# Norm weights spread into PSUM by TensorE, one-value operations as tensor_scalar, and one product for branch B's meta tokens

## The chip, the cores and the metric

The kernel runs on one core of a Trainium2 chip. The core has TensorE (matmul; its weight loads are shown as an engine of their own), VectorE (DVE), ScalarE (ACT), GpSimd (POOL) and SyncE, whose queue (SP) issues most of the transfers from and to the chip's memory. The metric is the device time of one execution in microseconds (us); a kernel's time is the median of several runs.

## The reference

One layer of a bidirectional encoder: 16 meta tokens are put ahead of 1024 tokens of width 1024; the rows are normalised, projected into ten blocks of columns, run through two attention branches, gated, mixed and normalised again. Cut to what the change touches:

```python
def rmsnorm(x, g):
    y = x * lax.rsqrt(jnp.mean(x * x, axis=-1, keepdims=True) + EPS)
    return y * g

h = concatenate([meta_tokens, x])                      # 16 + 1024 rows
hn = rmsnorm(h, pre_norm_g)
qa, ka, va, za, qb, kb, vb, zb, ga, gb = split(hn @ w_in + b_in)
oa = diff_attention(qa, ka, va, ...)                   # branch A: dense, 4 heads, two maps each
ob = windowed_gqa(qb, kb, vb, ...)                     # branch B: each block of 128 queries sees 3 blocks of keys
ya = (oa * silu(za)) @ w_out_a
yb = (ob * silu(zb)) @ w_out_b
h = h + rmsnorm((sigmoid(ga) * ya + sigmoid(gb) * yb) @ w_out, post_norm_g)
return h[16:]
```

In branch B only the first block of queries has the 16 meta tokens among its keys.

## The kernel before

All products keep fp32 accuracy by splitting operands into a rounded high part (fp32r) and the remainder: `hi*hi + hi*lo + lo*hi`. The weight splits run on POOL (L139, L140 in `load_w`), the splits of activations on ACT (high part) and DVE (remainder).

**Start.** The nine row blocks (block 0, block 1, the meta tokens as block -1, then 2 to 7) are each loaded by the SP queue (`load_x`, `ld` at L116), normalised (`norm_block`) and transposed (`turn_block`). `norm_block` squares on ACT with a row sum (L237), works out one value per row in `rstd` (sqrt on ACT at L161; on DVE L162 and L163, then L164 and L165 as `scalar_tensor_tensor` on 128x1 tiles) and applies it with the weights in one DVE pass over 128x1024 (L239). The weights `gb` are a 128x1024 tile in SBUF that one broadcast transfer of 512 KB fills. `turn_block` transposes eight 128x128 pieces on TensorE (L251) into two PSUM tiles (pool `psT` for the first four, `psS` for the others), and ACT (L254) and DVE (L255) write the parts into `hn`. Meanwhile `prepare` and `tables` make the bias tables (L272 on POOL, L283 on TensorE into `psS` banks, L284 on ACT).

**First projections.** As row blocks become ready, `k_proj`, `v_proj` and `q_proj` of branch B take chunks of columns: K and V in chunks of 264, 264, 256 and 256, Q in two of 512. Each chunk is 24 products (L151) into one bank of the two-bank pool `psmm`, then an evacuation (K: two ACT passes L328 and two DVE passes L332; V: one ACT pass L347; Q: L309 to L313). The row work has priority over the projections in the order that is laid out for each engine; that order is fixed when the kernel is built, and each engine follows its own in order. PSUM has eight banks: `psmm` 2, `psT` 2, `psV` 1, `psS` 3. An x tile is one of five buffers, and the load of a later block waits until the L239 pass of an earlier one has read its buffer.

**Branch B.** For each of four pairs of heads and eight query blocks: scores, softmax, transposes (`b_trans`, L432), and the value products (`b_values`, L445), six a step: three key blocks, each with the high and the low part of the probabilities. For query block 0 the third key block is the 16 meta rows, held in `VBM`, 16 partitions.

**After it.** Branch A (L585 to L629), in which L629 multiplies an 80-row tile `am` by an 80-row `VM` whose unused rows are zero, so that one product covers the meta rows' high and low parts; then gates, mixing, and the output stage, whose eight row blocks call `rstd` again (after the one-value sums L1056 and L1062). In branch A L596 is a one-value `tensor_tensor` once a step, 32 in all.

Of the kernel before, what the change touches and what calls it, by code (L numbers as in the profile page):

```python
# [17 lines left out]
P = 128  # L18
# [60 lines left out]
def _body(ctx, tc, A, out, dbg, stop):  # L79
# [35 lines left out]
    def ld(o, i):  # L115
        return sp.dma_start(o, i)  # L116
# [42 lines left out]
    def rstd(ss, st, n=P):  # L159

        act.activation(st[:n, 0:1], ss, AF.Sqrt, scale=4.0 / D, bias=eps4[:n])  # L161
        dve.tensor_scalar(st[:n, 3:4], ss, -4.0 / D, -4.0 * EPS, ALU.mult, ALU.add)  # L162
        dve.reciprocal(st[:n, 1:2], st[:n, 0:1])  # L163
        dve.scalar_tensor_tensor(st[:n, 4:5], st[:n, 1:2], st[:n, 3:4], st[:n, 1:2], ALU.mult, ALU.mult)  # L164
        dve.scalar_tensor_tensor(st[:n, 2:3], st[:n, 4:5], 3.0, st[:n, 1:2], ALU.add, ALU.mult)  # L165
        return st[:n, 2:3]
# [25 lines left out]
    VB_ = vt()  # L192
    VBM = sbp.tile([MT, 2, P], F32R, tag="am", name="vbm", bufs=1)
    xts = {}
# [13 lines left out]
    pool.memset(rb[32:33], 1.0)  # L208
    oh = [sbp.tile([33, LT // 2], F32, tag="U", name="oh") for _ in range(2)]
    load_x(0)  # L210
    act.dma_start(rb[:32], A["rel_bias"])
# [3 lines left out]
    load_x(-1)  # L215
    gb = sbp.tile([P, D], F32, tag="Q", name="gb", bufs=2)
    ld(gb, A["pre_norm_g"].partition_broadcast(P).rearrange("p o d -> p (o d)"))

# [13 lines left out]
    def norm_block(b):  # L232
        n = MT if b < 0 else P
        xt = xts.pop(b)
        xs = sbp.tile([P, D], F32, tag=("ah", "al")[b % 2], name="xs")
        st = sbp.tile([P, 8], F32, tag="st", name="st", bufs=9)
        pins[act] = act.activation(xs[:n], xt[:n], AF.Square, accum_out=st[:n, 5:6])  # L237
        r = rstd(st[:n, 5:6], st, n)
        pins[dve] = dve.scalar_tensor_tensor(xs[:n], xt[:n], r, gb[:n], ALU.mult, ALU.mult)  # L239
        xss[b] = xs  # L240
# [34 lines left out]
    def tables():  # L275
        for j in range(2):
            hot = hots[j]
            tab = sbp.tile([12, half], F32, tag="U", name="tab")
            for s in range(0, half, 512):
                w = min(512, half - s)  # L280
                pb = psS.tile([P, 512], F32, tag="s", name="pb")
                for x in range(2):
                    pe.matmul(pb[:12, :w], lhsT=rbs[:, x], rhs=hot[:, s:s + w], start=(x == 0), stop=(x == 1))  # L283
                act.activation(tab[:, s:s + w], pb[:12, :w], AF.Copy, scale=8.0)  # L284
            act.dma_start(tab_d[:, j * half:(j + 1) * half], tab)
# [4 lines left out]


    def zeros(*x):
        z = sbp.tile([P, 256], F32, tag="sq", name="zero", bufs=1)[:80]
        pool.memset(z, 0.0)
        for y in x:
            pool.tensor_scalar(y, z[:, :y.shape[1]], 1.0, 1.0, ALU.mult, ALU.mult)

    vm = [sbp.tile([80, P], F32R, tag=f"vm{j}", name=f"vm{j}", bufs=1) for j in range(2)]

    def masks():  # L300
        zeros(*vm)
        onesm = sbp.tile([P, 256], F32, tag="sq", name="onesm", bufs=1)[:, :P]
        pool.memset(onesm, 1.0 / P)
        pool.tensor_scalar(onesr, onesm, 1.0, 1.0, ALU.mult, ALU.mult)

    def q_proj(col, Q, w=None):
        def evac(ps, st, n, b):
            o = st - MT
            act.activation(Q[:64, 0, o:o + n], ps[:64, :n], AF.Identity, bias=b[:64])  # L309
            act.activation(Q[64:, 1, o:o + n], ps[64:, :n], AF.Identity, bias=b[64:])  # L310
            dve.scalar_tensor_tensor(Q[64:, 0, o:o + n], ps[:64, :n], b[:64], Q[:64, 0, o:o + n],
                                     ALU.add, ALU.subtract)
            dve.scalar_tensor_tensor(Q[:64, 1, o:o + n], ps[64:, :n], b[64:], Q[64:, 1, o:o + n],  # L313
                                     ALU.add, ALU.subtract)
        yield from proj(col, QCH, evac, w)

    def k_proj(col, KH, KL, w=None):
# [6 lines left out]
        def evac(ps, st, n, b):  # L324
# [10 lines left out]
            if w is not None and st + n in (SPLIT, C):  # L335
                copies(st + n - 512 - MT * (st < SPLIT), st + n)
        yield from proj(col, KCH if w is None else KCH4, evac, w)
        if w is None:
# [3 lines left out]
    def v_proj(col, put, w=None):  # L342
# [7 lines left out]
        yield from proj(col, KCH if w is None else KCH4, evac, w)  # L350
        for b0, nb, rows in ((0, 4, P), (4, 4, P), (8, 1, MT)):
# [20 lines left out]
    def put_b(VB):  # L372
        def put(pt, b0, nb, rows):
            for g in range(2):
                src = pt[:, :, 64 * g:64 * g + 64]
                v = VB[g][:, b0:b0 + nb] if b0 < 8 else VBM[:, g:g + 1]
                hi = v[:, :, :64]
                act.activation(hi, src, AF.Copy)
                dve.tensor_tensor(v[:, :, 64:], src, hi, ALU.subtract)
        return put  # L380
# [39 lines left out]
    def b_trans(i, sb):  # L420
        ah = sbp.tile([P, 4, 256], F32R, tag="ah", name="ah")
        al = sbp.tile([P, 4, 256], F32R, tag="al", name="al")
        if i == 0:
            blocks = ((17, P, 0), (17 + P, P, 1), (1, MT, 8))
        else:
            blocks = tuple((1 + P * j, P, i - 1 + j) for j in range(3 if i < NB - 1 else 2))
        for x in range(0, len(blocks), 2):
            pt = psT.tile([P, 2, 256], F32, tag="pT", name="pT")
            sub = blocks[x:x + 2]
            for y, (o, rows, _) in enumerate(sub):  # L430
                for j in range(2):
                    pe.transpose(out=pt[:rows, y, j * P:(j + 1) * P], in_=sb[:, j, o:o + rows], identity=ident)  # L432
            rows, n = sub[0][1], len(sub)
            act.activation(ah[:rows, x:x + n], pt[:rows, :n], AF.Copy)
            dve.tensor_tensor(al[:rows, x:x + n], pt[:rows, :n], ah[:rows, x:x + n], ALU.subtract)
        return ah, al, blocks

    def b_values(i, ah, al, blocks, g, ob):
        VB = VB_[g]
        pv = psV.tile([P, 512], F32, tag="pv", name="pv")  # L440
        n, last = 0, 2 * len(blocks) - 1
        for a in (ah, al):
            for x, (_, rows, blk) in enumerate(blocks):
                v = VB[:rows, blk, :] if blk < 8 else VBM[:, g, :]
                pe.matmul(pv[:, :256], lhsT=v, rhs=a[:rows, x, :], start=(n == 0), stop=(n == last))  # L445
                n += 1

        t = sbp.tile([P, 256], F32, tag="sq", name="bt", bufs=1)[:64]
# [126 lines left out]
    def a_scores(i, Q, KH, KL, U, fill):  # L575
# [104 lines left out]

    am = sbp.tile([80, 256], F32R, tag="am", name="am", bufs=1)
    zeros(am)
    U = a_table(0)
# [340 lines left out]
    with tc.tile_pool(name="fp", bufs=2, side="right", reuse_waits="tile") as fp:  # L1024
# [4 lines left out]
        def out_pair(p):  # L1029
# [13 lines left out]
            def result(o, v, cs):  # L1043
# [17 lines left out]
                if last:  # L1061
                    dve.tensor_tensor(s[:, 5:6], s[:, 5:6], s[:, 8:9], add)  # L1062
                if sqrt[0]:
# [44 lines left out]
```

## Time and profile before

| | us |
|---|---|
| median of 3 runs | 909.49 (909.27 to 910.65) |
| the profiled execution | 907.95 |
| its span on the core | 906.1 |
| TensorE busy in the span | 858.2 (95%) |
| DVE busy | 680.0 (75%) |
| ACT busy | 488.8 (54%) |
| POOL busy | 380.4 (42%) |

The span is what the trace covers; the profiled execution took 1.85 us more than its span. An engine counts as busy while an instruction of its own is in progress, and that includes time in which the instruction is held up inside the engine. In the page's 40 slices of 22.7 us TensorE is below 90% in four only: the first two, the one from 566 us, and the last.

### The profile page before, as it was taken

Reading aid. Unit: us, or ns where it says so; the run is one execution under the profiler, and the core shown is the slowest. Engines: PE = TensorE matmul, PEld = TensorE weight load, DVE = VectorE, ACT = ScalarE, POOL = GpSimd, SP = SyncE. Lnnn points to the kernel's source line nnn. Section 1 sums busy time; section 2 is a strip of 40 time slices with the busy share of each in tenths; the row PEclk is TensorE's granted clock in tenths of the full one; section 3 lists DMA queues with packets and bytes.
Section 4 is the critical chain, followed back from the end, with each engine's and each line's share of the span. In section 5 each row is a group of like instructions: output and inputs, shape, how many; then the busy total and the mean of one; then the engine's idle time right before and its main releaser. Section 6 shows DMA issues by size and latency. Waiting matters only on the chain.

```text
span 906.1 us, 13766 instructions
## 1 busy us (share of the span) xinstructions
PE 858.2 (95%) x4670; PEld 733.9 (81%) x4670; DVE 680.0 (75%) x1432; ACT 488.8 (54%) x975; POOL 380.4 (42%) x482
## 2 busy tenths in 40 slices
PE   4799999999999999999999999399999999999995
PEld 2797988888888898899888887288888888887784
DVE  6735668767988988997877699975444476959897
ACT  4635567766868768877766532344444540114432
POOL 6224543545021212221222189555454555826553
PEclk9999999999999999999999999699999999999998
DMA  8321110215122121021111153464511366311223
GB/s 262 105 50 45 56 57 19 89 43 133 36 71 68 47 72 68 25 71 48 47 65 48 47 185 117 163 210 161 178 56 47 131 231 207 94 63 47 94 95 138
DMA packets 64318, 85.85 MB, mean 95 GB/s; under 512 B 5248, under 2 KB 49294, under 8 KB 64248
## 3 DMA queue, kind: packets, MB, share of 16 engines
q1 hardware_dynamic: 56640, 60.28, 21.1%
q10 hardware_dynamic: 7576, 24.67, 7.9%
q8 instruction: 37, 0.61, 0.3%
q14 instruction: 33, 0.27, 0.1%
q0 software_dynamic: 32, 0.02, 0.0%
HBM read 60.63 MB, written 19.00 MB: 88 GB/s over the span
## 4 chain that ended last, share of the span: by engine, by line
PE 63%; DVE 21%; ACT 7%; issue 5%; POOL 1%; DMA 1%; SPq 0%; DVEq 0%; ACTq 0%; POOLq 0%
PE mm L151 21%; PE pp L862 17%; PE pp L966 9%; PE pv L627 3%; DVE sb L588 3%; PE pv L445 2%; PE pT L432 2%; PE pT L615 2%; PE s L585 2%; DVE sb L598 2%; ACT sb L591 2%; PE s L586 2%; ACT sb L597 1%; DVE ws L837 1%; DVE TB L885 1%
## 5 line engine op out<-in xcount | busy, mean ns | idle before, releaser
L151 PE MATMUL mm<-hn,wh 128*128 128x512 f32 (+2 forms) x896 | 203.6, 356 | 2.9 <-ACT vT L347 1.9
L139 POOL TENSOR_SCALAR wh<-wr 128x256 fp32r<-128x256 f32 x124 | 63.5, 528 | 265.9 <-PE mm L151 237.4
L151 PEld LDWEIGHTS mm<-hn,wh 128*128 128x128 f32 x896 | 145.1, 192 | 19.2 <-ACT vT L347 2.1
L140 POOL TENSOR_TENSOR wl<-wr,wh 128x256 fp32r<-128x256 f32 x124 | 107.4, 890 | 19.4 <-PE mm L151 17.4
L151 PE MATMUL mm<-hn,wl 128*128 128x512 f32 (+2 forms) x448 | 101.5, 353 | 0.0
L792 POOL TENSOR_TENSOR wl<-ws,wh 128x512 fp32r<-128x512 f32 x48 | 71.6, 1501 | 66.0 <-ACT wh L791 52.2
L591 ACT ACTIVATE sb<-sb,st 128x1040 f32<-128x1040 f32 x64 | 74.3, 1162 | 35.2 <-DVE st L588 34.4
L862 PE MATMUL pp<-t,wh 128*128 128x512 f32 (+1 forms) x296 | 73.2, 390 | 15.6 <-ACT wh L791 15.6
L862 PE MATMUL pp<-hn,wh 128*128 128x512 f32 x320 | 79.8, 391 | 0.0
L151 PEld LDWEIGHTS mm<-hn,wl 128*128 128x128 f32 x448 | 73.7, 191 | 7.6
L862 PEld LDWEIGHTS pp<-t,wh 128*128 128x128 f32 x296 | 55.5, 191 | 28.2 <-ACT wh L791 16.9
L588 DVE CUSTOM_DVE_ANT_0 sb<-s,U,st 128x346 f32<-128x346 f32 x128 | 73.1, 574 | 5.8
L871 DVE TENSOR_TENSOR c<-c,pp 128x512 f32<-128x512 f32 x70 | 47.4, 682 | 38.5 <-PE pp L862 36.7
L862 PEld LDWEIGHTS pp<-hn,wh 128*128 128x128 f32 x320 | 60.1, 188 | 13.2
L585 PE MATMUL s<-K,Q 128*128 128x346 f32 (+1 forms) x192 | 65.8, 345 | 0.9 <-DVE st L588 0.4
L586 PE MATMUL s<-K,Q 128*128 128x346 f32 (+1 forms) x192 | 61.3, 321 | 0.0
L598 DVE SCALAR_TENSOR_TENSOR sb<-sb,st 128x1040 f32<-128x1040 f32 x32 | 43.9, 1372 | 13.2 <-ACT sb L597 12.9
L413 ACT ACTIVATE sb<-sb,st 128x385 f32<-128x385 f32 (+2 forms) x64 | 37.5, 588 | 22.6 <-DVE st L410 20.3
L417 POOL TENSOR_SCALAR sb<-sb,st 128x384 f32<-128x384 f32 (+2 forms) x64 | 35.5, 568 | 32.5 <-DVE st L415 32.4
L791 ACT ACTIVATE wh<-ws 128x512 fp32r<-128x512 f32 x48 | 29.7, 625 | 35.0 <-PE pp L862 20.1
L410 DVE CUSTOM_DVE_ANT_0 sb<-s,TB,nsink 128x384 f32<-128x384 f32 (+2 forms) x64 | 35.4, 580 | 16.6 <-PE s L408 15.0
L617 DVE TENSOR_TENSOR al<-pT,ah 128x512 fp32r<-128x512 f32 x64 | 43.7, 686 | 3.6 <-ACT ah L616 2.9
(212 smaller groups left out, 1928.7 us busy)
## 6 DMA issues: line engine op xcount, KB each, us to landing
wr<-in_w_in_dram SPq DMA_DIRECT2D x96, 128.0 KB, 2.5
wr<-in_w_in_dram SPq DMA_DIRECT2D x16, 512.0 KB, 3.6
K<-K ACTq DMA_DIRECT2D x16, 260.0 KB, 3.5
xt<-in_x_dram SPq DMA_DIRECT2D x8, 512.0 KB, 7.1
sg_d<-TB ACTq DMA_DIRECT2D x8, 512.0 KB, 2.6
w<-in_w_out_dram SPq DMA_DIRECT2D x4, 1024.0 KB, 5.5
room<-sg_d SPq DMA_DIRECT2D x8, 512.0 KB, 4.8
fx<-in_x_dram SPq DMA_DIRECT2D x8, 512.0 KB, 4.6
```

Of the source, the lines that this page charges most:

```text
L139: pool.tensor_scalar(hi, raw, 1.0, 1.0, ALU.mult, ALU.mult)
L140: pool.tensor_tensor(lo, raw, hi, ALU.subtract)
L151: pe.matmul(ps[:, :n], lhsT=w[k // 4][:, k % 4, :], rhs=hslice(part, k, st, n), start=(i == 0), stop=(i == 3 * KC - 1))
L585: pe.matmul(s, lhsT=q, rhs=KH[:, m, o:o + n], start=True, stop=False)
L586: pe.matmul(s, lhsT=q, rhs=KL[:, m, o:o + n], start=False, stop=True)
L588: dve.tensor_tensor_reduce(out=sb[:, o:o + n], in0=s, in1=back(U, u0 + o, n), scale=-0.125, scalar=lim, op0=ALU.add, op1=ALU.min, accum_ou ...
L591: act.activation(sb, sb, AF.Exp, bias=st[:, m:m + 1], scale=-1.0, accum_out=st[:, 2 + m:3 + m])
L598: dve.scalar_tensor_tensor(sbs[0], sbs[0], st[:, 4:5], sbs[1], ALU.mult, ALU.add)
L792: lo_eng.tensor_tensor(t[1][:, k], x, t[0][:, k], sub)
L862: pe.matmul(x[n][:, cs], lhsT=w[:, k], rhs=b[n][part][:, k, cs], start=(i == 0), stop=(i == 11))
L871: dve.tensor_tensor(x[o][:, cs], *src, add)
L966: pe.matmul(py, lhsT=w[:, k, :], rhs=g[h][:, k], start=(i == 0), stop=(i == 11))
```

## The change

Four things change.

1. The weights of the first norm are loaded as one row of 4 KB (on ACT's queue, ahead of the other loads of that queue), split on DVE into a high and a low part, and spread over the 128 partitions by four TensorE products with a row of ones, into the two `psmm` banks, which they keep until the last norm. L239 becomes two passes of 512 columns that read the weights from PSUM. The table products move from `psS` to the one bank of `psV`, and the first projections (`beside(w)`) take their banks from `psS` instead of `psmm`.
2. L164 and L165 in `rstd`, L596, L1056 and L1062 become `tensor_scalar` with the second and third value as scalars per partition.
3. Branch B's meta rows are kept twice in an 80-row `VBM` (rows 0 to 15 and 64 to 79, zeros between) and the probabilities' high and low parts in the matching rows of `am`, so that one product replaces two. The value tile is written by twice as many small ACT and DVE passes, once.
4. `am` and `VBM` are zeroed in `masks` with the others, and no longer `am` ahead of branch A.

```diff
-        dve.scalar_tensor_tensor(st[:n, 4:5], st[:n, 1:2], st[:n, 3:4], st[:n, 1:2], ALU.mult, ALU.mult)
-        dve.scalar_tensor_tensor(st[:n, 2:3], st[:n, 4:5], 3.0, st[:n, 1:2], ALU.add, ALU.mult)
+        dve.tensor_scalar(st[:n, 4:5], st[:n, 1:2], st[:n, 3:4], st[:n, 1:2], ALU.mult, ALU.mult)
+        dve.tensor_scalar(st[:n, 2:3], st[:n, 4:5], 3.0, st[:n, 1:2], ALU.add, ALU.mult)
...
-    VBM = sbp.tile([MT, 2, P], F32R, tag="am", name="vbm", bufs=1)
+    VBM = sbp.tile([80, 2, P], F32R, tag="sh", name="vbm", bufs=1)
...
+    grow = sbp.tile([1, D], F32, tag="Q", name="grow", bufs=2)
+    act.dma_start(grow, A["pre_norm_g"])
...
-    gb = sbp.tile([P, D], F32, tag="Q", name="gb", bufs=2)
-    ld(gb, A["pre_norm_g"].partition_broadcast(P).rearrange("p o d -> p (o d)"))
+    one = sbp.tile([1, P], F32, tag="sq", name="one", bufs=1)
+    dve.memset(one, 1.0)
+    oner = sbp.tile([1, P], F32R, tag="vm0", name="oner", bufs=1)
+    dve.tensor_copy(oner, one)
+    gr = sbp.tile([1, 2, T], F32R, tag="Q", name="gr", bufs=2)
+    dve.tensor_copy(gr[:, 0], grow)
+    dve.tensor_tensor(gr[:, 1], grow, gr[:, 0], ALU.subtract)
+    gb = [psmm.tile([P, 512], F32, tag="mm", name="gb") for _ in range(2)]
+    for h in range(2):
+        for x in range(2):
+            pe.matmul(gb[h], lhsT=oner, rhs=gr[:, x, 512 * h:512 * h + 512], start=(x == 0), stop=(x == 1))
...
-        pins[dve] = dve.scalar_tensor_tensor(xs[:n], xt[:n], r, gb[:n], ALU.mult, ALU.mult)
+        for h in range(2):
+            c = slice(512 * h, 512 * h + 512)
+            pins[dve] = dve.scalar_tensor_tensor(xs[:n, c], xt[:n, c], r, gb[h][:n], ALU.mult, ALU.mult)
...
-                pb = psS.tile([P, 512], F32, tag="s", name="pb")
+                pb = psV.tile([P, 512], F32, tag="pv", name="pb")
...
+    def beside(w):
+        return {"room": lambda: psS.tile([P, 512], F32, tag="s", name="mm")} if w else {}
...
-        yield from proj(col, KCH if w is None else KCH4, evac, w)
+        yield from proj(col, KCH if w is None else KCH4, evac, w, **beside(w))
...
+        if i == 0:
+            pe.matmul(pv[:, :256], lhsT=VBM[:, g, :], rhs=am, start=False, stop=True)
...
-        dve.tensor_tensor(st[:, 6:7], st[:, 5:6], neglam, ALU.mult)
+        dve.tensor_scalar(st[:, 6:7], st[:, 5:6], neglam, None, ALU.mult)
...
-                    dve.tensor_tensor(s[:, 5:6], s[:, 6:7], s[:, 7:8], add)
+                    dve.tensor_scalar(s[:, 5:6], s[:, 6:7], s[:, 7:8], None, add)
```

## Rows read from the trace of the kernel before

**Rows 1.** Windows of the start: busy us of each engine, instructions, granted clock, DMA.

```profile
10.00:20.00 10.00, 8.32 (x29) 4.27 (x30) 9.96 (x16) 5.11 (x11) 9.09 (x13) 1.00 0.74 248
...
30.00:41.50 11.50, 9.65 (x64) 9.41 (x64) 9.90 (x29) 9.35 (x22) 0.00 (x0) 1.00 0.42 121
```

**Rows 2.** TensorE's waits from 41.5 to 240 us: us in total, times, longest.

```profile
PE mm L151 <- ACT vT L347: 1.9, 1, 1.9
```

**Rows 3.** Chain of waits, first 50 us: start us, us, what.

```profile
2.11 6.80 DMA gb<-in_pre_norm_g_dram
...
17.09 5.51 DVE st L164
...
22.82 1.28 DVE xs L239
...
30.00 4.49 PE mm L151 x19
```

**Rows 4.** Timeline of POOL, 12 to 23 us, first and last of eight rows.

```profile
12.14 1.73 POOL L139 TENSOR_SCALAR wh<-wraw 128x256 fp32r<-128x256 f32 x2
...
21.18 1.40 POOL L140 TENSOR_TENSOR wl<-wraw,wh 128x256 fp32r<-128x256 f32 x2
```

**Rows 5.** Timeline of DVE, 0 to 32 us.

```profile
3.88 0.17 DVE L268 CAST rbs<-rb 33x12 fp32r<-33x12 f32 x1 [3.88 <-DMA rb<-in_rel_bias_dram]
...
12.21 4.12 DVE L239 SCALAR_TENSOR_TENSOR xs<-xt,st,gb 128x1024 f32<-128x1024 f32 x2
16.25 0.13 DVE L162 TENSOR_SCALAR st<-st 128x1 f32<-128x1 f32 x1
16.32 0.67 DVE L255 TENSOR_TENSOR hn<-pt,hn 128x512 fp32r<-128x512 f32 x1
```

**Rows 6.** Timeline of TensorE, start.

```profile
11.86 1.88 PE L283 MATMUL pb<-hot,rbs 33*12 33x512 f32 x4
...
30.00 3.01 PE L151 MATMUL mm<-hn,wh 128*128 128x264 f32 x12 [0.66 <-ACT hn L254]
...
35.32 1.62 PE L151 MATMUL mm<-hn,wh 128*128 128x264 f32 x12
```

**Rows 7.** Waits of the SP queue, first 60 us.

```profile
SPq L116 <- DVE xs L239: 11.6, 2, 7.4
```

**Rows 8.** Evacuation of K's first chunk, timelines of ACT and DVE.

```profile
36.41 0.96 ACT L328 ACTIVATE K<-mm,binT 64x264 fp32r<-64x264 f32 x2
...
38.16 0.99 DVE L332 SCALAR_TENSOR_TENSOR K<-mm,binT,K 64x264 fp32r<-64x264 f32 x2
```

**Rows 9.** Timeline of TensorE: branch B's value products, and branch A's 80-row product.

```profile
85.56 0.40 PE L445 MATMUL pv<-ah,V 128*128 128x256 f32 x2
...
86.95 0.50 PE L151 MATMUL mm<-hn,wh 128*128 128x512 f32 x1
...
93.05 0.52 PE L445 MATMUL pv<-ah,V 128*128 128x256 f32 x3
...
93.77 0.82 PE L432 MATMUL pT<-ident,sb 128*128 128x128 f32 x6
...
245.49 0.28 PE L629 MATMUL pv<-am,vm 80*128 80x256 f32 x1
245.61 0.27 PE L607 MATMUL pT<-ident,sb 128*16 128x128 f32 x1
```

**Rows 10.** Output stage: DVE and POOL side by side, and TensorE's waits after 830 us.

```profile
867.28 2.58 POOL L792 TENSOR_TENSOR wl<-ws,wh 128x512 fp32r<-128x512 f32 x2 [1.32 <-PE pp L862]
...
867.39 0.15 DVE L162 TENSOR_SCALAR fs<-fs 128x1 f32<-128x1 f32 x1
...
867.92 0.68 DVE L164 SCALAR_TENSOR_TENSOR fs<-fs 128x1 f32<-128x1 f32 x1
...
PE pp L862 <- ACT wh L791: 1.3, 3, 0.6
```

**Rows 11.** L164 in the whole trace: ns min/median/max, first and last start us, forms.

```profile
L164 DVE SCALAR_TENSOR_TENSOR st<-st x9: 200/219/5502, 6.3 to 41.8; 128x1 f32<-128x1 f32 x8, 16x1 f32<-16x1 f32 x1
```

More of the change, by code (lines that the diff above doesn't have):

```diff
@@ L295, in zeros @@
         for y in x:
+            y = y.rearrange("p a b -> p (a b)") if len(y.shape) == 3 else y
             pool.tensor_scalar(y, z[:, :y.shape[1]], 1.0, 1.0, ALU.mult, ALU.mult)
+    am = sbp.tile([80, 256], F32R, tag="am", name="am", bufs=1)
     vm = [sbp.tile([80, P], F32R, tag=f"vm{j}", name=f"vm{j}", bufs=1) for j in range(2)]
     def masks():
-        zeros(*vm)
+        zeros(*vm, VBM, am)
         onesm = sbp.tile([P, 256], F32, tag="sq", name="onesm", bufs=1)[:, :P]
@@ L314, in evac @@
                                      ALU.add, ALU.subtract)
-        yield from proj(col, QCH, evac, w)
+        yield from proj(col, QCH, evac, w, **beside(w))
     def k_proj(col, KH, KL, w=None):
@@ L349, in evac @@
                 pinned(act, x)
-        yield from proj(col, KCH if w is None else KCH4, evac, w)
+        yield from proj(col, KCH if w is None else KCH4, evac, w, **beside(w))
         for b0, nb, rows in ((0, 4, P), (4, 4, P), (8, 1, MT)):
@@ L375, in put @@
                 src = pt[:, :, 64 * g:64 * g + 64]
[L376 to L379, printed above, removed]
+                for r in (0, 64)[:1 if b0 < 8 else 2]:
+                    v = VB[g][:, b0:b0 + nb] if b0 < 8 else VBM[r:r + MT, g:g + 1]
+                    hi = v[:, :, :64]
+                    act.activation(hi, src, AF.Copy)
+                    dve.tensor_tensor(v[:, :, 64:], src, hi, ALU.subtract)
         return put
@@ L423, in b_trans @@
         if i == 0:
-            blocks = ((17, P, 0), (17 + P, P, 1), (1, MT, 8))
+            blocks = ((17, P, 0), (17 + P, P, 1))
         else:
@@ L432, in b_trans @@
                     pe.transpose(out=pt[:rows, y, j * P:(j + 1) * P], in_=sb[:, j, o:o + rows], identity=ident)
-            rows, n = sub[0][1], len(sub)
+            rows, n = P, len(sub)
             act.activation(ah[:rows, x:x + n], pt[:rows, :n], AF.Copy)
             dve.tensor_tensor(al[:rows, x:x + n], pt[:rows, :n], ah[:rows, x:x + n], ALU.subtract)
+        if i == 0:
+            pt = psT.tile([P, 2, 256], F32, tag="pT", name="pT")
+            for j in range(2):
+                pe.transpose(out=pt[:MT, 0, j * P:(j + 1) * P], in_=sb[:, j, 1:1 + MT], identity=ident)
+            act.activation(am[:MT], pt[:MT, 0], AF.Copy)
+            dve.tensor_tensor(am[64:80], pt[:MT, 0], am[:MT], ALU.subtract)
         return ah, al, blocks
@@ L440, in b_values @@
         pv = psV.tile([P, 512], F32, tag="pv", name="pv")
-        n, last = 0, 2 * len(blocks) - 1
+        n, last = 0, 2 * len(blocks) - (i > 0)
         for a in (ah, al):
             for x, (_, rows, blk) in enumerate(blocks):
-                v = VB[:rows, blk, :] if blk < 8 else VBM[:, g, :]
-                pe.matmul(pv[:, :256], lhsT=v, rhs=a[:rows, x, :], start=(n == 0), stop=(n == last))
+                pe.matmul(pv[:, :256], lhsT=VB[:rows, blk, :], rhs=a[:rows, x, :], start=(n == 0), stop=(n == last))
                 n += 1
+        if i == 0:
+            pe.matmul(pv[:, :256], lhsT=VBM[:, g, :], rhs=am, start=False, stop=True)
         t = sbp.tile([P, 256], F32, tag="sq", name="bt", bufs=1)[:64]
@@ L679, in a_step @@
             late.append(values)
-    am = sbp.tile([80, 256], F32R, tag="am", name="am", bufs=1)
-    zeros(am)
     U = a_table(0)
@@ L1061, in result @@
                 if last:
-                    dve.tensor_tensor(s[:, 5:6], s[:, 5:6], s[:, 8:9], add)
+                    dve.tensor_scalar(s[:, 5:6], s[:, 5:6], s[:, 8:9], None, add)
                 if sqrt[0]:
```

## The prediction

> **What bounds the kernel now.** I read the busy shares first: TensorE is in use for 95% of the span, and of the 40 slices only the first two, one near 570 us and the last are not full. So an edit counts if it brings forward the moment from which TensorE runs without a gap, if it takes work from TensorE in the full stretch, or if it shortens the end after the last product. Next, windows of the start [rows 1]: from 10 to 20 us TensorE is busy 8.3 us with 29 instructions, from 30 to 41.5 us 9.7 with 64, so it is short of work in both, while DVE counts as busy for all of 10 to 20 us with no more than 16 instructions. TensorE's waits after 41.5 us [rows 2] then show one of 1.9 us and two others of 0.2 up to 240 us: from 41.5 us on, branch B is bound by TensorE, and whatever moves 41.5 earlier moves everything behind it, the stall near 570 us included, since that one follows the end of branch A.
>
> The chain of waits tells what made 41.5 so late [rows 3]: the broadcast weights land at 8.9 us, one `scalar_tensor_tensor` on a 128x1 tile (L164, block 2) holds DVE from 17.09 to 22.60, block 2's norm pass follows, and the first long run of products starts at 30.0. The timelines say why L164 took 5.5 us: POOL runs weight splits without a pause from 12.14 to 22.58 [rows 4], and L164 ends as POOL does. In the same stretch, two norm passes (one of them on 16 rows) took 4.12 us together [rows 5], while a `tensor_scalar` took 0.13 and a PSUM-and-SBUF `tensor_tensor` (L255) 0.67 beside the same POOL work. So what waits is the DVE instruction with two SBUF tensors, however small.
>
> **The change part by part.**
>
> *The norm's weights.* The row of 4 KB should be there at about 3.9 us, as the 1.5 KB transfer that now stands first on that queue is [rows 5]. Two DVE passes over 1024 values follow, each at most the 1.28 us of a full norm pass [rows 3]: 6.5 us. Four products of 512 columns at 0.47 [rows 6] give the first half at about 7.0 and the second at 7.9. Block 0's value per row is ready by about then (now its pass waits for the weights alone, to 8.9), so the pass runs from about 7.1 to 8.7 instead of 9.05 to 10.33: 1.6 us earlier. Each pass becomes two halves of about 0.7, taken from L255's 0.67 for the same shape with one PSUM input [rows 5]; nine passes cost DVE at most 9 x 0.12 = 1.1 us more, beside work that it no longer stalls in. The 512 KB transfer goes from the SP queue, which brings block 2 and the weights behind it forward by up to 2.1 us at the 248 GB/s of [rows 1].
>
> *The stalls of the first norms.* Beside POOL, block 1 and the meta rows then take 2.8 us in place of 4.12, and block 2's L164 0.2 in place of 5.5. Laid out anew: the meta pass ends at about 13.8 (now 16.3), block 0's two remainders and block 2's one-value steps take 2.1, block 2's pass 1.4: 17.3, where it now ends at 24.1. That is **6.8 us** on the chain. Behind it stands a second delay: between 24.1 and 30.0 TensorE transposes block 2 and the second half of the meta rows, which in this order come that late because table products hold `psS` banks. With the tables in `psV` the meta rows can be turned ahead of block 2, and after 17.3 only block 2's eight transposes (2 us at the slow pace) are left: dense from 19.3, **10.7 us** earlier. The weight splits, which POOL also does faster without DVE in its way, are done for K by then. Which of the two it is depends on the new order, which I can't see; I take 9, between them, because what limits behind it has room: x loads wait 11.6 us for norm passes [rows 7], a wait that shortens with them.
>
> Slow products: at 30.0 twelve products of 264 columns took 3.01 us, at 35.3 twelve took 1.62 [rows 6], at a granted clock of 1.00 (2.4 GHz) in both [rows 1]. I leave this in place at the new dense start; should TensorE pause again between blocks, another dozen slow products would cost 1.4 us.
>
> *Banks.* The norm weights keep `psmm` until block 7's pass, so first projections share three `psS` banks with half of the transposes. A K chunk hands its bank back after two ACT and two DVE passes: from 36.41 to 39.15, 2.7 us [rows 8]. If TensorE has the other two banks to go on with, this is hidden; if not, it is idle for that long. Ten chunks are concerned. I count one such exposure inside the 9, and the rest as a rival. `psV` with one bank makes six table pieces go one by one, in a stretch where TensorE has nothing else, and only branch B's scores read the tables.
>
> *Meta rows in one product.* In the four steps of query block 0 the six value products take 85.56 to 86.95 = 1.39 us, while six of 128 rows take 93.05 to 93.77 = 0.72 [rows 9]; the 16-row shape is what costs. The 80-row product of branch A takes 0.12 from start to start [rows 9]. So 1.39 becomes 5 x 0.12 = 0.60, saving 0.79, and four steps **3.2 us** of a stretch where TensorE is the bound. The value tile's extra ACT and DVE passes (two each, on 16x64) lie beside the projections; they are smaller than K's passes of 0.5 [rows 8], so they cost at most 2 us if that cover were gone. Zeroing adds two POOL instructions behind the first norms, at most 0.87 each by the split passes of [rows 4], and takes one away later; TensorE waits for POOL in none of the rows after 41.5 [rows 2].
>
> *One-value steps later.* In the output stage a `tensor_scalar` took 0.15 while POOL's split ran from 867.28, and L164 just after it took 0.68, up to the end of the first of the two POOL instructions [rows 10]. Such stalls go, but TensorE waits for only 1.3 us in all after 830 [rows 10]: a gain of 0 to 0.9. Behind the last product, four one-value steps stand in a row. With scalars per partition one should lie between the 0.13 of a `tensor_scalar` with constants [rows 5] and the 0.22 that is usual for L164 [rows 11], so at most 4 x 0.09 = 0.4 is lost. I take 0. L596, 32 times, lies beside a full TensorE: 0.
>
> *Sum:* 9.0 + 3.2 + 0 = 12.2 us. The profiled execution took 907.95 (span 906.1 and 1.85 around it), so 895.75 for one like it; the median of the runs lies 1.54 above that execution, so 909.49 - 12.2 = **897.3**.
>
> **The rivals.**
>
> *It doesn't do what it says.* A `tensor_scalar` that reads and writes SBUF might wait for POOL as well; then L164 and L165 keep their stalls, and what is left is 1.6 for the weights, 1.3 for the norm passes (4.12 to 2.8) and 3.2 for branch B: 903.4. Against it: [rows 5, 10], where `tensor_scalar` ran beside POOL in 0.13 and 0.15 and a stalled instruction stood right behind it. For it: those had constants, the new ones read further values from SBUF. The Trainium skill (SBUF — State Buffer, section "Who interferes with whom") has the rule that two SBUF inputs contend with POOL's reads, and there the trace agrees; it also lists `tensor_scalar` among the instructions that can take the shared ports in a faster mode and then block, which speaks against this edit, and there the two rows disagree with it for one value per partition. Chance 0.06.
>
> *Only the stall.* The order stays as it is behind block 2, or several bank hand-overs are exposed: the start gives 3 to 6.8, and with 3.2 the time is 899.5 to 903.3. For it: `psS` is now used by three kinds of work. Chance 0.17.
>
> *Slower.* Each of the ten chunks that wait for a bank leaves TensorE idle for the hand-over of 2.7 us, in the first 50 us. From 5 exposed (12.2 / 2.7 = 4.5) the gain is gone; all ten would give 897.3 + 27 = 924, seven 916. Against it: V chunks hand back after a single ACT pass, ready row blocks give TensorE transposes to do, and now the two `psmm` banks go through the same hand-overs with one exposed wait, the 1.9 of [rows 2]. Chance 0.04.
>
> *More.* TensorE gets K and V products as soon as blocks 0, 1 and the meta rows are turned, at about 17, and the 1.9 us wait of [rows 2] also goes: 12.7 and 3.2, with 0.5 in the output stage: 893.1. Against it: a block costs DVE 1.4 for the pass, 1.3 for two remainders and 0.6 for four small steps, so 13 us for blocks 2 to 5 behind that point. Chance 0.13.
>
> **How the numbers follow.** Forecast 0.60 (start 7 to 11: 895.3 to 899.3), more 0.13, only the stall 0.17, not what it says 0.06, slower 0.04. From 893.0 to 903.0 leaves out the slow cases, part of the one above and a little below: under 0.2. About 0.2% (1.8 us) is what a measurement of this kernel can tell from no change; faster 0.96, same 0.01 (four or five hand-overs exposed), slower 0.03.
>
> **What would show it.** Right: L164 and L165 at about 0.2 us in the first 25 us beside POOL; block 0's pass before 9 us; the first run of L151 near 19 to 21 us and TensorE full from about 32; the products L445 of query block 0 within 0.6 us; and every later stage earlier by the same 12. Wrong: stalls of one-value instructions that end as POOL's do; TensorE waiting in L151 for evacuations (L328, L332, L313) before 60 us; table products L283 with ACT's L284 between them ahead of the transposes L251; or a gain at 72 us that is gone by 580, which would mean that the stall there does not follow branch A.

## The result, and the profile after

| | before | after |
|---|---|---|
| median, us | 909.38 (908.74 to 910.65, 4 runs) | 901.29 (900.47 to 902.2, 4 runs) |
| profiled execution, us | 907.95 | 902.2 |
| its span, us | 906.1 | 900.4 |
| TensorE busy in the span, us | 858.2 | 859.1 |

The ratio is 0.9908, 95% interval 0.9893 to 0.9922: 8.1 us gained, where 12.2 were forecast (897.3). The two profiled executions are only 5.75 us apart, since the one of before lies 1.4 below its median and the one of after 0.9 above. Stages below are compared between profiles, sizes of whole edits between medians.

The starts of the same products in both traces (first score of branch B, first score and last value product of branch A, first product of the gate's projection after it, first of the output mix, last product, span) give the ledger, with differences taken before rounding:

| | before | after | difference so far | of this stage |
|---|---|---|---|---|
| first score, branch B | 73.1 | 69.8 | -3.3 | -3.3 |
| first score, branch A | 211.1 | 205.4 | -5.7 | -2.3 |
| last values, branch A | 519.8 | 514.4 | -5.4 | +0.3 |
| first L862 / L888 | 560.5 | 555.2 | -5.2 | +0.2 |
| first L966 / L992 | 730.3 | 726.2 | -4.1 | +1.1 |
| last product | 895.9 | 891.0 | -4.8 | -0.7 |
| span | 906.1 | 900.4 | -5.7 | -0.9 |

So the start gave 3.3 where 9 were forecast, branch B 2.3 where 3.2 were, and the output stage 1.6 where 0 was taken. First the timeline of DVE (start, duration, instruction), in the stretch of the old stall:

```profile
14.88 0.66 DVE L269 TENSOR_TENSOR hn<-pt,hn 128x512 fp32r<-128x512 f32 x1
15.47 0.25 DVE L164 TENSOR_SCALAR st<-st 128x1 f32<-128x1 f32 x1
...
17.11 0.73 DVE L253 SCALAR_TENSOR_TENSOR xs<-xt,st,gb 128x512 f32<-128x512 f32 x1
17.76 0.27 DVE L164 TENSOR_SCALAR st<-st 128x1 f32<-128x1 f32 x1
...
24.17 0.15 DVE L162 TENSOR_SCALAR st<-st 128x1 f32<-128x1 f32 x1 [3.25 <-ACT xs L249]
28.73 0.15 DVE L162 TENSOR_SCALAR st<-st 128x1 f32<-128x1 f32 x1 [4.41 <-ACT xs L249]
```

The stall is gone: L164 takes 0.25 to 0.27 beside POOL's splits, a half of a norm pass (now L253) 0.73, and block 2's pass ends at 17.84 where it ended at 24.1 and 17.3 was forecast. But then DVE is idle for 3.25 and 4.41 us, for ACT's squares (L249). The timelines of TensorE, ACT and POOL say why:

```profile
20.09 1.25 POOL L286 TENSOR_SCALAR hot<-oh 33x1288 fp32r<-33x1288 f32 x1
...
21.40 1.03 PE L297 MATMUL pb<-hot,rbs 33*12 33x512 f32 x2 [1.34 <-POOL hot L286]
22.36 1.11 PE L265 MATMUL pt<-ident,xs 128*128 128x128 f32 x4
...
22.51 0.59 ACT L298 ACTIVATE tab<-pb 12x512 f32<-12x512 f32 x1 [3.11 <-POOL wq L140]
23.01 1.04 ACT L249 ACTIVATE xs<-xt 128x1024 f32<-128x1024 f32 x1
...
27.08 0.59 ACT L298 ACTIVATE tab<-pb 12x512 f32<-12x512 f32 x1 [2.94 <-PE pb L297]
27.57 1.04 ACT L249 ACTIVATE xs<-xt 128x1024 f32<-128x1024 f32 x1
```

POOL's second copy of the onehot, at 10.91 before, now stands behind all splits of K's and V's weights, at 20.09. The table products (L297) wait for it in TensorE's queue, with block 2's transposes (L265) behind them, which could have run from 17.84; each table piece holds the one bank of `psV` until ACT's copy L298, and ACT, itself in order, is idle for 3.11 and 2.94 us in front of those copies with the squares of blocks 4 and 5 behind them. The windows show the outcome beside [rows 1] (busy us of TensorE, its weight loads, DVE, ACT and POOL, then the granted clock):

```profile
10.00:20.00 10.00, 7.75 (x32) 4.46 (x30) 8.81 (x25) 6.46 (x15) 9.30 (x16) 1.00 1.03 336
20.00:30.00 10.00, 8.66 (x33) 6.01 (x33) 1.60 (x7) 3.35 (x7) 5.74 (x10) 1.00 0.32 93
30.00:41.50 11.50, 10.32 (x77) 9.76 (x78) 10.69 (x32) 8.31 (x19) 2.24 (x8) 1.00 0.26 77
```

From 20 to 30 us DVE and ACT do 1.60 and 3.35 us of work in 10, and TensorE counts as busy for 8.66 with only 33 instructions.

### The profile page after: what moved, and what is told of

It reads as the page before. It is cut to its first block, busy times and chain, and to the rows that moved or that the text cites. A ratio compares the mean times of both kernels' runs of the same rounds, so it can differ in the third digit from the quotient of the medians.

```text
span 900.4 us, 13792 instructions
## 1 busy us (share of the span) xinstructions
PE 859.1 (95%) x4670; PEld 733.5 (81%) x4670; DVE 672.2 (75%) x1447; ACT 491.1 (55%) x977; POOL 381.2 (42%) x482
## 4 chain that ended last, share of the span: by engine, by line
PE 67%; DVE 17%; ACT 6%; issue 5%; POOL 3%; DMA 1%; DVEq 0%; ACTq 0%; POOLq 0%
PE mm L151 21%; PE pp L888 17%; PE pp L992 9%; PE pv L655 4%; PE s L613 3%; PE pT L643 3%; PE s L614 2%; PE pT L453 2%; POOL wl L818 2%; DVE sb L616 2%; DVE sb L626 2%; PE pv L471 2%; DVE TB L911 1%; ACT sb L625 1%; ACT sb L619 1%
## 5 line engine op out<-in xcount | busy, mean ns | idle before, releaser
L151 PE MATMUL mm<-hn,wh 128*128 128x512 f32 (+2 forms) x896 | 203.1, 356 | 0.9 <-DVE Q L333 0.9
L151 PEld LDWEIGHTS mm<-hn,wh 128*128 128x128 f32 x896 | 144.9, 191 | 16.8 <-issue 1.2
L140 POOL TENSOR_TENSOR wl<-wr,wh 128x256 fp32r<-128x256 f32 x124 | 109.5, 905 | 20.4 <-PE mm L151 18.4
L151 PE MATMUL mm<-hn,wl 128*128 128x512 f32 (+2 forms) x448 | 101.2, 353 | 0.0
L888 PE MATMUL pp<-t,wh 128*128 128x512 f32 (+1 forms) x296 | 73.4, 391 | 15.2 <-ACT wh L817 15.2
L151 PEld LDWEIGHTS mm<-hn,wl 128*128 128x128 f32 x448 | 73.5, 191 | 7.9 <-issue 0.4
L888 PE MATMUL pp<-hn,wh 128*128 128x512 f32 x320 | 79.8, 391 | 0.0
L888 PEld LDWEIGHTS pp<-t,wh 128*128 128x128 f32 x296 | 55.7, 192 | 27.5 <-ACT wh L817 16.0
L888 PEld LDWEIGHTS pp<-hn,wh 128*128 128x128 f32 x320 | 60.1, 188 | 13.2
L613 PE MATMUL s<-K,Q 128*128 128x346 f32 (+1 forms) x192 | 66.2, 347 | 0.4 <-DVE st L616 0.2
```

The source lines that it names most:

```text
L140: pool.tensor_tensor(lo, raw, hi, ALU.subtract)
L151: pe.matmul(ps[:, :n], lhsT=w[k // 4][:, k % 4, :], rhs=hslice(part, k, st, n), start=(i == 0), stop=(i == 3 * KC - 1))
L613: pe.matmul(s, lhsT=q, rhs=KH[:, m, o:o + n], start=True, stop=False)
L888: pe.matmul(x[n][:, cs], lhsT=w[:, k], rhs=b[n][part][:, k, cs], start=(i == 0), stop=(i == 11))
```

## The experiments

All times are medians with the ratio to the kernel before on the same chip. A second mark of the start is the first product with Q's weights: 49.2 before, 44.2 after.

### Which part did what

**After without the one-value operations** (parts 1 and 3 stay):

```diff
-        dve.tensor_scalar(st[:n, 4:5], st[:n, 1:2], st[:n, 3:4], st[:n, 1:2], ALU.mult, ALU.mult)
+        dve.scalar_tensor_tensor(st[:n, 4:5], st[:n, 1:2], st[:n, 3:4], st[:n, 1:2], ALU.mult, ALU.mult)
...
```

> The kernel after with the one-value operations put back as scalar_tensor_tensor and tensor_tensor with two SBUF inputs; the weights in PSUM and the meta product stay. Theory 'the one-value operations are what ends the stall': L164 of one of the blocks is held for 3 us or more in the first 23 us and ends as POOL's series does, and the time is 903 to 907. Rival 'the path has moved': after is held by the tables' place in the queues, so the stall is hidden behind that and the time stays within 1 us of after's 901.3. Second rival 'the weights alone do it': no stall over 1 us at all.

Measured: 902.82, 0.9927 [0.9911, 0.9944], 1.5 us above after. Timelines of DVE and POOL in this run:

```profile
10.55 1.27 DVE L164 SCALAR_TENSOR_TENSOR st<-st 128x1 f32<-128x1 f32 x1
...
16.91 0.35 DVE L164 SCALAR_TENSOR_TENSOR st<-st 128x1 f32<-128x1 f32 x1
...
20.08 1.21 DVE L164 SCALAR_TENSOR_TENSOR st<-st 128x1 f32<-128x1 f32 x1
...
10.56 1.26 POOL L286 TENSOR_SCALAR hot<-oh 33x1288 fp32r<-33x1288 f32 x1 [1.93 <-DMA oh<-in_onehot_dram]
...
20.02 1.26 POOL L286 TENSOR_SCALAR hot<-oh 33x1288 fp32r<-33x1288 f32 x1
```

With two SBUF inputs L164 again ends as a POOL instruction does (11.82 and 11.82, 21.29 and 21.28), but at the end of one instruction, not of a series (L165 once got past the rest of one and a second, 0.88 us): at the start no hold is over 1.27 us. The first score of branch B comes at 69.9, as in after (69.8). So part 1 ends the long stall without the one-value form (part 3 doesn't: in its own run, below, L164 is held for 5.51 us), and at the start that form adds nothing. Part 1 puts the weights into PSUM and also changes the order; no run tells the two apart. The 1.5 us lie elsewhere: from the first mix product to the end this run takes 176.0, before 175.8, after 174.2. That is the output stage.

**Before with the one-value operations alone** (part 2):

> The kernel before, with the one-value operations alone as tensor_scalar. If the stall of L164 was simply 5.5 us on the chain: about 903 (5.5 for block 2, 0.9 at the end). If it moves to the next instruction with two SBUF inputs (block 2's pass L239, weights still in SBUF, POOL busy to 22.6): block 2's pass ends near 23.9 instead of 24.1, and the time is 908 to 909.5.

Measured: 907.35 (903.4 to 910.36), 0.9971 [0.9954, 0.9989]: 2.4 us, and more spread than any other kernel here. From first mix product to end it takes 174.2, so the 1.6 of the output stage are there. At the start L164 takes 0.27, and the hold moves on to the next instruction with two SBUF inputs, block 2's norm pass:

```profile
15.43 0.27 DVE L164 TENSOR_SCALAR st<-st 128x1 f32<-128x1 f32 x1
15.74 0.21 DVE L165 TENSOR_SCALAR st<-st 128x1 f32<-128x1 f32 x1
15.87 0.68 DVE L255 TENSOR_TENSOR hn<-pt,hn 128x512 fp32r<-128x512 f32 x1
16.47 8.02 DVE L239 SCALAR_TENSOR_TENSOR xs<-xt,st,gb 128x1024 f32<-128x1024 f32 x1
```

In this execution that was longer than the 5.50 of [rows 11], and branch B's first score came 2.1 later than before (75.1). Here this part alone only changed the victim. But the traced execution, at 909.78, is the second slowest of nine; the fastest took 903.4, close to the 903 expected with no hold at all, so how long the hold was in the others isn't shown.

**Before with the meta product alone** (part 3):

> The kernel before with nothing but branch B's meta tokens in one 80-row product (no change to the norm's weights, none to one-value operations). Theory: the four steps of query block 0 lose 0.76 us each in a stretch where TensorE is the bound, as in the trace of after, and nothing else changes: 909.5 - 3.05 = 906.4. Rival (the product isn't on the path, or the extra evacuations cost it): within 1 us of before. Should it be 907.5 or more, less than two thirds of the 3.05 reach the end.

Measured: 908.47 (906.69 to 909.41), 0.999 [0.9981, 1.0]: 0.8 us, not 3. In the traces branch B, from its first score to its last, takes 134.4 instead of 136.4, so 2.0 of the products' 3.07 reach the end of the stage. TensorE's waits in that stretch, in this run (us in total, times, longest):

```profile
PE mm L151 <- DVE Q L315: 0.8, 3, 0.3
PE pv L453 <- DVE ob L461: 0.5, 2, 0.3
PE pT L357 <- DVE al L438: 0.3, 1, 0.3
PE pT L435 <- POOL sb L420: 0.2, 1, 0.2
```

1.8 us in sum, where before had two of 0.2. With TensorE ahead by 3, DVE's evacuations of Q and of the outputs become late. Another 0.8 goes behind the stall near 570 us, below.

### What held the start

**The row of weights on SP's queue** (so that the onehot loads and POOL's copies come early again):

```diff
-    act.dma_start(grow, A["pre_norm_g"])
+    ld(grow, A["pre_norm_g"])
```

> The changed kernel, but the row of norm weights is loaded on the SP queue instead of ACT's. Theory 'order': the row at the head of ACT's queue pushed the second one-hot load from 4.5 to 11.2 us, POOL's second copy from 10.9 to 20.1, and with it the second half of the tables to 21 to 30 us, where ACT, in order, holds the squares of blocks 4 and 5 behind them (DVE waits 3.3 and 4.4 us for them). With the row on SP the second copy is back near 10 us, the squares come by 20 us, and the start is 4 to 5 us earlier: 896 to 898 against 901.3. Theory 'one bank' (the tables one by one in psV): the pieces still go one by one, 900 to 902. Theory 'hand-over' (first projections share psS): no gain, 901.

Measured: 902.14, 0.9914 [0.9897, 0.993], no gain. POOL's copies are back ahead of the splits (6.07 and 10.34), but the squares of blocks 0 and 1, which wait for x, start at 6.23 and 10.07 instead of 4.22 and 6.11, behind the row and the onehot; ACT takes both ahead of block 0's square root, so that block's pass runs from 12.31, and the tables still go one by one with ACT's copies between the squares (those of blocks 4 and 5 at 26.29 and 28.88). The late copy isn't the whole cause; undoing it here was paid for by a late x.

**Tables in `psS` again**:

```diff
-                pb = psV.tile([P, 512], F32, tag="pv", name="pb")
+                pb = psS.tile([P, 512], F32, tag="s", name="pb")
```

> The changed kernel, but the table products go back from the one bank of psV to the three of psS. Theory 'one bank': table products no longer wait for ACT one by one, 3 to 5 us earlier, 897. Theory 'order': the second copy on POOL still comes at 20 us, so the second half of the tables still holds ACT then: 900 to 903. Theory 'hand-over': a third kind of work in psS makes it worse, 903 or more.

Measured: 903.25, 0.9926 [0.9911, 0.9941]. More banks don't help, because the wait for POOL's copy stays. In TensorE's timeline the run with three banks puts the tables of the first half through in one go, and then stands before the second half:

```profile
21.87 2.31 PE L297 MATMUL pb<-hot,rbs 33*12 33x512 f32 x6 [5.26 <-POOL hot L286]
24.12 2.51 PE L265 MATMUL pt<-ident,xs 128*128 128x128 f32 x12
```

**Tables behind the last norm**, everything else as in after:

```diff
             with tc.high_priority(150):
                 prepare()
-                tables()
-            TB = b_table(0)
...
+        if j == 6:
+            tables()
+            TB = b_table(0)
     masks()
```

> The changed kernel, but the tables are made after block 5's norm and without priority, still in psV, with the row still on ACT's queue. Theories 'order' and 'one bank' both say that the tables' place in ACT's order costs the start, so the start gains 3 to 5 us: 896 to 898. Theory 'hand-over': 901, and block 4's squares come no earlier or bring nothing.

Measured: 898.41, 0.9874 [0.9859, 0.9889]. Once more, beside the runs further down:

> The kernel after with nothing but its table products behind the last norm, once more, beside the two runs with extra products on one chip. 898.4 within 1 us, so that it stays ahead of after's 901.3; at 900 or more the two are one.

Measured: 897.42, 0.9872 [0.9855, 0.9889]. These are 2.9 and 3.9 below after, and no kernel here is faster by more than its runs spread. Timelines of TensorE and ACT in the second one:

```profile
17.02 2.13 PE L151 MATMUL mm<-hn,wh 128*128 128x264 f32 x8 [1.05 <-ACT hn L268]
...
20.63 1.04 ACT L249 ACTIVATE xs<-xt 128x1024 f32<-128x1024 f32 x1
...
21.67 1.04 ACT L249 ACTIVATE xs<-xt 128x1024 f32<-128x1024 f32 x1
```

The squares of blocks 4 and 5 come 2.4 and 5.9 us earlier than in after, Q's first product at 38.0 instead of 44.2. Not all of the tables are late: eight of the twelve products still run before 32 us, where the order has room for them, but of ACT's copies only two (17.44 and 20.14) are ahead of those squares, the third comes at 27.36. So the place of the tables in the two in-order queues is what kept the start from giving more.

**The same on before**:

> The kernel before with nothing but its table products moved behind the last norm, as in the run of after with late tables that took 898.4. Theory 'what the tables cost is uncovered by the change': before, the stall of L164 covers them, so at most 1 us is gained: 908.5 to 910. Rival 'the tables cost the same in both': 3 us are gained here too, 906.5, and then the change itself was worth no less than I took and the tables are a matter of their own.

Measured: 905.39, 0.9957 [0.9941, 0.9973]: 3.9 us gained. My theory here fell. I had held that the stall of L164 hid what the tables cost; L164 is held for 6.90 us in this run and the tables still cost as much. Timelines of DVE and POOL:

```profile
16.72 6.90 DVE L164 SCALAR_TENSOR_TENSOR st<-st 128x1 f32<-128x1 f32 x1
...
23.22 0.40 POOL L139 TENSOR_SCALAR wq<-wr 128x256 fp32r<-128x256 f32 x1
23.70 0.74 POOL L140 TENSOR_TENSOR wq<-wr,wq 128x256 fp32r<-128x256 f32 x1
```

The gain is that of the medians. The traced execution (906.24) is at the upper end of the four and only 1.7 below that of before, and the first score (60.4) is no mark here, since 268 products of TensorE stand ahead of it instead of 333.

The tables are a matter of their own, and the change itself is worth about the same with them late (905.39 to 898.41, 7.0) as with them early (8.1).

**Onehot loads, POOL's copies and tables all late:**

> The kernel after with the onehot loads (behind the x loads, on SP's queue), POOL's two copies of them and the table products all behind the last norm. Against the run with late products alone (898.4): POOL's weight splits end 1.3 us earlier, TensorE does four products of 512 columns (2.0 us at the slow pace) later and at the fast one, block 1's x no longer shares the DMA engines with 340 KB of onehot. Theory 'queues': first long run of L151 near 15.5 and 1 to 2.5 us better, 896 to 897.5. Rival 'slow products': the run of products starts earlier but goes at 0.25 us for 264 columns until about the same time as before, so under 1 us is gained, 897.5 to 898.5.

Measured: 900.75, 0.9908 [0.9893, 0.9922], worse than late products alone. POOL's splits did end early (16.7), but nothing that TensorE needed came sooner: the copy of the bias, which the first evacuation of K waits for, moved from 9.99 to 25.16 in DVE's order, the squares of blocks 4 and 5 went behind it, to 26.4 and 27.5, and between two waits of 2.7 and 1.4 us TensorE's granted clock fell to 0.62 (15 to 20 us) and 0.70 (20 to 25). An edit that only removes work from the front also moves everything that the order fills in.

### The slow products

**Nine products of ones ahead of everything** (kernel with late tables; they go to a bank that nobody reads):

```diff
...
+    def warm(n):
+        pw = psV.tile([P, 512], F32, tag="pv", name="pw")
+        for y in range(n):
+            pe.matmul(pw, lhsT=wb[:, :P], rhs=wb, start=True, stop=True)
+
+    warm(9)
```

> The kernel with late tables (898.4) plus nine products of 128x128 by 512 columns of ones into a bank that nobody reads, ahead of the norm weights' products, while TensorE has nothing else; the order of all other products stays. In the run without them, 26 products of L151 between 16.7 and 26 us went at 0.25 to 0.27 us for 264 columns, against 0.135 later, and transposes at 0.24 against 0.15, at a granted clock that reads 1.00. Theory 'the slow pace is a matter of how long TensorE has run products': with nine ahead, the weights' products and the transposes of block 0 go at the fast pace from about 7 us; if that lasts, the 26 products lose 3 us, 895.5. Rival 'it falls back': what TensorE does between 9 and 16 us (transposes, tables, pauses) isn't enough to hold the pace, L151 starts slow at 16.7 as before, and the time stays at 898.4 within 1 us. Rival 'it isn't a pace of TensorE' (the weights or operands arrive slowly): the nine products change neither.

Measured: 898.38, 0.9879 [0.9863, 0.9896]: nothing. The rival is right, and the trace says more. Windows of this run:

```profile
10.00:15.00 5.00, 3.97 (x16) 2.39 (x14) 4.46 (x18) 2.52 (x5) 4.09 (x7) 0.50 1.08 341
15.00:20.00 5.00, 3.94 (x19) 2.86 (x18) 4.41 (x14) 2.97 (x8) 4.92 (x10) 0.50 1.00 311
20.00:25.00 5.00, 5.00 (x26) 3.90 (x26) 3.33 (x13) 4.32 (x10) 4.75 (x8) 0.65 0.45 135
```

The last two of them in the run without these products (late tables, the second one):

```profile
15.00:20.00 5.00, 3.95 (x19) 2.79 (x18) 4.90 (x15) 2.97 (x8) 4.92 (x10) 1.00 0.92 284
20.00:25.00 5.00, 5.00 (x27) 4.04 (x27) 3.32 (x13) 4.46 (x10) 4.75 (x8) 1.00 0.52 153
```

With the nine products the granted clock falls to 0.50 (1.2 GHz) at 10 us, while TensorE does transposes with pauses, and stays there until about 23. Without them the record reads 1.00 all the while, and yet the work goes at the very same pace: eight products of L151 in 2.13 us in both runs, the fast pace in both from 23.5. So at the start 1.00 in the windows doesn't say 2.4 GHz; the pace of the products does, and the slow products of [rows 6] went at the pace of the lower clock too.

**Such products behind the transposes of blocks 0, 1 and the meta rows as well:**

> The run before this one plus two more such products behind each half of the transposes of blocks 0, 1 and the meta rows; this also moves the order (block 2's transposes come ahead of the first L151, tables later). Theory 'pace': L151's first run goes at 0.135 us for 264 columns; twelve extra products cost 2.6 us before 17 us, partly in TensorE's pauses, and up to 3 us come back behind: 894.5 to 898. Rival 'they are only in the way': the pace stays at 0.25, and the time rises to 899.5 to 901.

Measured: 898.03, 0.988 [0.9862, 0.9898]. Now the first run of L151 is fast:

```profile
20.44 2.18 PE L151 MATMUL mm<-hn,wh 128*128 128x264 f32 x16
```

0.136 us each, at a granted clock of 1.00 from 15 us on, but it begins at 20.4 instead of 17.0. Q's first product comes 2.7 us earlier than without the extra products (35.3), the first score only 0.7 (64.1), and branch A's first score not at all (200.4 in both): ten table products now stand in the full stretch behind 45 us, where the run without extra products has four, and did the others in TensorE's pauses; the six more take 1.4 us from start to start.

**The same behind blocks 0 and 2 only:**

> The same products of ones, nine in front and two behind each half of the transposes of blocks 0 and 2 alone (eight in place of twelve, none behind the meta rows, where six of them held TensorE from 16.1 to 18.3 us). Theory 'the pace was right, the delay ate it': L151 starts near 18 to 19 instead of 20.4, at 0.135 us for 264 columns, and the first scores come at about 63 instead of 64.1 to 64.8: 896 to 897. Rival 'the clock isn't held by so few': L151's first products go at 0.25 as without them, 897.5 to 899. Rival 'TensorE isn't the bound of the first norms': it starts no earlier than 20 since blocks come from DVE and ACT at their own pace, 897.5 to 898.5.

Measured: 900.0, 0.9901 [0.9885, 0.9918]. L151 starts at 20.50, at the fast pace, Q's first product at 36.0, and the first score at 66.9, 2 us later than with no extra products at all. Here twelve table products stand in the full stretch, 2.0 us more than with four, and the one bank of `psV` shows its price, in TensorE's timeline:

```profile
61.67 0.63 PE L313 MATMUL pb<-hot,rbs 33*12 33x512 f32 x2 [1.26 <-ACT tab L314]
```

What the higher clock gives at the start (up to 2.7 us) is lost again, for the most part by what gets out of TensorE's pauses. No version with the extra products was faster than late tables alone by more than the runs spread.

## Why the prediction was right or wrong

**The norm's weights: right.** Block 0's pass ran from 8.27 to 9.7 (7.1 to 8.7 forecast), halves took 0.73 to 0.75, block 2's pass ended at 17.84 (17.3).

**The stalls of the first norms: gone as forecast, but another part is enough for it.** I gave 5.3 of the 6.8 us to the one-value form ("what waits is the DVE instruction with two SBUF tensors, however small"). The rule holds for a single POOL instruction, as the run without that form shows, but with part 1 L164 waits 1.27 at most at the start, in either form the start ends alike, and with the one-value form alone the hold went to the norm pass (8.02) in the one execution that was traced. The rival *it doesn't do what it says* is out: L164 as `tensor_scalar` with further values from SBUF took 0.25 to 0.28 in every run, beside POOL or not. The Trainium skill (SBUF — State Buffer, section "Who interferes with whom") lets `tensor_scalar` block on POOL in a faster mode, where its operands meet certain conditions; for one value per partition no run here shows that, and its rule on two SBUF inputs agrees with the 1.27 that ends with POOL's instruction.

**"Behind it stands a second delay ... I take 9": this step failed.** It measured 3.3 at the first score. Two things were wrong in it. The first is what the 10.7 above it counts: the stretch from 19.3 to 30.0 as if TensorE had been empty there. Windows of before, from 20 to 30 us and from 10 us to the first score:

```profile
20.00:30.00 10.00, 6.09 (x25) 4.00 (x24) 5.93 (x8) 2.92 (x9) 7.12 (x13) 1.00 0.60 192
10.00:73.10 63.10, 55.54 (x333) 46.72 (x333) 38.20 (x78) 28.11 (x59) 26.77 (x49) 1.00 0.42 124
```

TensorE was busy for 6.1 of those 10 us, with work that has to be done in any order, and idle for 7.6 from 10 us to the first score, so its waits there didn't hold 9. The same stretch in after:

```profile
10.00:69.80 59.80, 54.90 (x331) 45.89 (x329) 31.51 (x81) 29.01 (x59) 26.45 (x51) 1.00 0.41 120
```

And with late tables, the second run:

```profile
10.00:64.80 54.80, 52.90 (x332) 44.70 (x331) 31.90 (x86) 28.72 (x59) 26.40 (x51) 1.00 0.45 126
```

Idle are 4.9 and 1.9: the change took 2.7 of the 7.6 away, and the place of the tables held 3.0 of the rest. That place is the second thing, in the sentence on `psV`: the tables one by one, "in a stretch where TensorE has nothing else", were costed at nothing, and I had listed "table products L283 with ACT's L284 between them ahead of the transposes" as what would show me wrong. That is what came. I looked at TensorE, where the tables had room, and not at ACT, whose copies stand in one queue with the squares, nor at POOL's copy of the onehot, whose new place behind 8 us of splits was a change of order that the diff doesn't show. Late tables give 2.9 to 3.9 back. The number of the rival *only the stall* (899.5 to 903.3) was met, but neither of its two causes: no evacuation of a first chunk kept TensorE waiting (one hand-over did, of a bank of transposes, 1.2 us at 36.1), and the order behind block 2 did change. That 901.3 is still inside 893 to 903 is in part luck, since the output stage gave 1.6 that I had not counted.

**The slow products: left in place as forecast, but read wrongly.** I took the 1.00 of the windows for 2.4 GHz at both paces; the slow one is the pace of the lower clock, which lasts from the first product to 23 to 27 us with late tables. In after 25 products of L151 up to 30.6 us went slowly, 0.22 from start to start against 0.12, about 2.4 us, but before had 26 of them, up to 33.9, so they are no part of what the start fell short by.

**Meta rows in one product: mechanism right, size off.** The four steps lost 3.06 (3.2 forecast): 81.91 to 82.52 is one of them, in place of [rows 9]:

```profile
81.91 0.41 PE L471 MATMUL pv<-ah,V 128*128 128x256 f32 x2
82.15 0.41 PE L471 MATMUL pv<-al,V 128*128 128x256 f32 x2
82.39 0.29 PE L474 MATMUL pv<-am,vbm 80*128 80x256 f32 x1
82.52 0.85 PE L151 MATMUL mm<-hn,wh 128*128 128x512 f32 x3
```

But 2.0 to 2.3 of it reach the end of branch B, since DVE's evacuations are then late, and 0.8 the end of the kernel when it stands alone.

**"Every later stage earlier by the same 12": nearly.** What branch B had gained was still there at 555 us (-5.2 after -5.7). The stall of 14.7 us near 570 is unchanged, but how long the clock stays low behind it is not. The window of 575 to 585 us in before:

```profile
575.00:585.00 10.00, 4.11 (x12) 3.32 (x13) 10.00 (x8) 2.92 (x5) 7.34 (x5) 0.56 0.49 164
```

The same window in after:

```profile
575.00:585.00 10.00, 9.33 (x30) 7.48 (x31) 8.22 (x8) 4.19 (x7) 9.30 (x6) 0.70 0.67 235
```

A mean of 0.70 between the levels 0.50 and 1.00 is 6 of 10 us at 0.50, a mean of 0.56 is 8.8. Without work TensorE was for 0.7 and 5.9 us of these, so it worked at 0.50 (1.2 GHz) for 5.3 us in after and 2.9 in before; at half the pace that is 1.2, the +1.1 of the ledger. From the first L862 to the first mix product the kernels took 169.8 to 171.3, without order by edit (before 169.9, after 171.0), and one and the same kernel, that with late tables, 170.5 and 171.2 in its two traces. So executions differ here by most of that without any edit, and the 1.1 can't be put down to the change.

**One-value steps later: underrated.** I took 0 out of 0 to 0.9; in the traces with part 2 the time from first mix product to end is 174.1 to 174.7 (174.2 in after), in those without 175.8 to 176.0. Of after's 1.6, 0.7 lie before the last product and 0.9 behind it. L164 in the output stage (ns min/median/max) before:

```profile
L164 DVE SCALAR_TENSOR_TENSOR fs<-fs x8: 214/464/1307, 841.2 to 901.1; 128x1 f32<-128x1 f32 x8
```

And after:

```profile
L164 DVE TENSOR_SCALAR fs<-fs x8: 268/271/275, 837.2 to 895.3; 128x1 f32<-128x1 f32 x8
```

The small loss that I allowed for is there too: the last L164 takes 0.27 instead of 0.22.

**What stays open.** Part 1 was never run alone: parts 1, 3 and 4 together gave 6.5 against before (902.82 to 909.3), part 3 with its share of 4 gave 0.8 alone and 2.3 by the end of branch B in after, so 4 to 6 for part 1 is worked out and not measured. Between the medians lie 8.1, between the profiles 5.7; where the other 2.4 lie can't be seen, since each of the two has one trace here. One source of such differences is shown: two executions with late tables had the fast pace begin at 27 and at 23.5 us, and the first score at 66.2 and 64.8. And why L164 gets in at the end of one POOL instruction with the weights in PSUM, but was passed over by a whole series in the kernels with the weights in SBUF (5.50, 5.51, 6.90, and 8.02 for the norm pass), no run tells. The traces show where the long holds end, at POOL's first pause: at 22.58 before, ahead of 23.85, and in the run of before with late tables at 23.62, ahead of 23.70. With part 1, L164 got in at 17.26 without such a pause.

## What to carry to other kernels

When a stall on one engine is taken away, go through every in-order queue of that stretch, ACT's and POOL's too, and ask what stands in front of the next thing needed: small side work such as a table is free on the engine with room and dear on the queue where it waits. Check edits one by one, since each part alone may only move a hold to the next instruction, and the part that was meant to end it need not be the one that does. Here 3 to 4 us more lay in the place of a few small products, and moving them found it, not adding banks. And bound what a stretch can give by the idle time of the limiting engine in it (7.6 us here), not by how much earlier its dense part begins (10.7).

## What the runs showed of the hardware that I had not expected

- A DVE instruction with two SBUF inputs can be held for one POOL instruction (1.27 us) or, in the kernels with the weights in SBUF, through a series of them (5.50, 5.51, 6.90, 8.02 us).
- The granted clock reads 1.00 before its first change in a record, also where the work goes at the pace of 0.50 (eight products of 264 columns in 2.13 us at either reading). After nine products in front it fell to 0.50 at 10 us, amid transposes and pauses; with four more such products among block 0's transposes it was at 1.00 from 15 us on.
- Removing 0.77 us per step from TensorE in a full stretch let other engines' evacuations come late: 3.07 us of shorter products became 2.0.
